# A hybrid decoder layer on one core: two more blocks of the up projection written into the fixed order, and the first down weights loaded into slots

## The chip, the core and the metric

The kernel runs on one core of a Trainium2 chip. The core has five engines that run side by side, each with its own list of instructions: TensorE (PE in the profile: matmuls, with its weight loads in a column PEld), VectorE (DVE), ScalarE (ACT), GpSimd (POOL) and SyncE (SP, here only a queue that issues transfers). Transfers are issued from the queues of SP, ACT and POOL. The metric is the device time of one execution in microseconds (us).

## The reference

One layer: a mixer (mLSTM heads and a causal convolution group, one output projection) and a causal ConvFFN, each between norms, with six modulation rows worked out from a condition vector. Batch 1, 512 positions, width 1024, all float32. The change lies in the ConvFFN:

```
u = rms_norm(x, ffn_pre_g) * (1.0 + sc2) + sh2
up = causal_dwconv(u @ ffn_up, ffn_conv_w, ffn_conv_b)     # 1024 -> 2 x 2816, 3 taps along the positions
a, gt = split(up, 2)
f = (silu(gt) * a) @ ffn_down                              # 2816 -> 1024
x = x + g2 * rms_norm(f, ffn_post_g)
```

## The kernel before, in words

**Numbers in two parts.** TensorE multiplies fp32r operands, so each operand is split into a high part (a copy to fp32r) and a low part (the rest), and each product is three matmuls: high x high, high x low, low x high (`mm3`, L186). A weight tile of 128 x 512 is split in one of two ways: `w_split` (L164) has ACT copy the high part and POOL subtract it for the low part (L170, L171); `added_split` (L1074) has ACT copy the high part, ACT copy it again with scale -1 into the low part (L1077, L1078), and a transfer issued by POOL add the source into the low part (L1079).

**Up projection.** The 2816 columns of each half are 22 units of 128 columns; unit i has a value half (a) and a gate half (g). Units 0 to 7 are plain: 48 matmuls of 512 columns into two PSUM banks (`plain_unit`, L1119). A unit's weights are one raw tile of 128 x 2048, loaded by SP into one of two raw places. From unit 8 on, units go in pairs, one pair a block (m = 4 to 10). The even unit i is computed by a Strassen-Winograd scheme with seven half-size products: sums of weight quarters a11, a12, a21, a22 (p1, p7, p5, p6, then p2, p3, p4) against sums of token quarters (t1 to t4, made once by `token_forms`, L1046, and kept in slots). TensorE's order in a block is written out: the first products p1, p7, p5, p6 into banks X, Z and W (48 matmuls of 256 columns), the value half of the odd unit j (24 of 512), the last products p2, p3, p4 (36 of 256), the gate half of j (24 of 512). Between the first and the last products, `between` (L1099) adds up X, Z and W: two copies on ACT and four operations on VectorE. It needs W, and the last products need it.

**Behind each half** comes a convolution with three taps (`conv3`, L992: one operation on ACT, two on VectorE), which reads the bank and so sets when it is free again; then `unit_out` (L1125: silu on ACT, product on VectorE) writes the half of a tile F. With both units of a pair done, `form_sums` (L1016) and `form_parts` (L1026) make the sums that the down projection multiplies, split them into four slots and spill the rest to memory (L1030, L1031). The first four pairs of sums go out to memory whole (`own_out`, L1138, four transfers from ACT's queue) and come back before the down projection needs them (`reload`, L1254).

**What sets the order.** SP's and TensorE's lists follow the program text. On ACT, VectorE and POOL a list scheduler with a timing model picks the order, except within `in_order()` (L49), where each of these engines keeps the order of the text; instructions from outside may still be put between those of the list. The list with `in_order()` for the up projection begins at L1173 and covers blocks 4 to 10. Before it, the plain units 0 to 7 with their sums (m = 0 to 3, L1150 to L1160) are left to the scheduler; behind it, so is the down projection.

**Places.** `slots` has 44 tiles of 128 x 512 that the scheduler hands out as they come free; `wpool` has 20 for split weights; `raws` two raw places; `mmbank` four PSUM banks, `cvbank` two, `atbank` two. Block 4's X and Z take two of the four mm banks, and unit 9's halves the two cv banks.

**Down projection.** Also Winograd, over 11 groups m of weights (order 4 to 10, then 0 to 3: `ORDER`, L1037). `load1` (L1288) loads three quarters of a group, in one transfer of 768 KB, `forms1` (L1292) makes three sums on VectorE, splits four tiles and writes one sum to memory for later. Groups 0 and 1 go into the raw places, 2 and 3 into the place of the up projection's activations `u2h` (`wd_raw`, L1275; tile `more`). The first phase multiplies p1, p5, p7, p6 of each group (`prod1`, L1331), six matmuls of 512 columns each; p5 and p7 take the mm banks, p6 the cv banks, so p7 wants the banks of unit 20 and p6 those of unit 21.

Of the kernel before, what the change touches and what calls it, by code (L numbers as in the profile page):

```python
# [52 lines left out]
def decoder_layer(ctx, tc, w_glu0, x, xT, c, adaT, vecs, w_glu, w_qko, w_v0, w_v, w_out, w_up, w_down, out):  # L53
# [33 lines left out]
    def mmbank(name):  # L87
        return psum.tile([P, T], F32, tag="mm", bufs=4, name=name)
# [1058 lines left out]
    def open_F(m):  # L1147
        Fs[m] = vpool.tile([P, 2 * T + 8], F32, tag="vh", name=f"F{m}")

    for m in range(MS):  # L1150
# [6 lines left out]
        form_sums(m, Fs[m])  # L1157
        form_parts(m, Fs[m])
        if m < SPILLED:
            own_out(m)  # L1160
    up_load(2 * MS, (0, 2, 3, 1))
    up_load(2 * MS + 1, range(4))
# [7 lines left out]
    def value_part(i, n):  # L1170
        return added_split(places(i)[n], f"wup{i}_{n}")

    with in_order():  # L1173
# [5 lines left out]
        V.tensor_tensor(out=a21, in0=a21, in1=a22, op=ALU.add)  # L1179
        weight_form(i, "p7", a11)  # L1180
        weight_form(i, "p5", a21)
        V.tensor_tensor(out=a11, in0=a22, in1=a11, op=ALU.subtract)
        weight_form(i, "p6", a11)
        value = [value_part(i + 1, n) for n in range(2)]
        before = None
        for m in range(MS, NM):
            i, j = 2 * m, 2 * m + 1
            more_to_come = m + 1 < NM
            open_F(m)
            banks = first_products(i)  # L1190
            pa = plain_half(cvbank(f"up{j}_0"), value, 0)
            s4 = slot(f"s4_{m}")
            V.tensor_tensor(out=s4, in0=a12, in1=a11, op=ALU.subtract)
            weight_form(i, "p2", a12, added_split)
            weight_form(i, "p4", a22)
            if before:
                bj, ba, bg = before
                bg = conv3(bg, NF + bj, f"fg{bj}")
# [4 lines left out]
            if before:  # L1203
                unit_out(bj, ba, bg, Fs[m - 1])
            gate = [value_part(j, 2)]
            if before:
                form_sums(m - 1, Fs[m - 1])
# [4 lines left out]
            if before:  # L1212
                form_parts(m - 1, Fs[m - 1])
# [45 lines left out]

    pairs = pairs[SPILLED:]  # L1260
    g2_d = [g2_d[m] for m in ORDER]
    w_down = [w_down[m] for m in ORDER]


    M1 = NM - 2
    M2 = NM - 3
# [8 lines left out]
    def wd_raw(m, n):  # L1275
        return raws.tile([P, 2048], F32, tag="raw", name=f"wd{n}_{m}") if m % 4 < 2 else more[:, m % 2, :]

    def parts(r, names):
        out = {}
        for name, b in names:  # L1280
            hi, lo = wpool.tile([P, T], F32R, tag="w", name=f"{name}h"), wpool.tile([P, T], F32R, tag="w", name=f"{name}l")
            split(r[:, b * T : (b + 1) * T], hi, lo)
            out[name[:2]] = (hi, lo)
        return out

    loaded = {}

    def load1(m):  # L1288
        loaded[m] = r = wd_raw(m, 1)
        nc.sync.dma_start(r[:, T:], w_down[m][:, T:])  # L1290

    def forms1(m):  # L1292

        r = loaded.pop(m)
        t3, b11, b12, b22 = (quarter(r, b) for b in range(4))
        V.tensor_tensor(out=t3, in0=b22, in1=b12, op=ALU.subtract)
        V.tensor_tensor(out=b12, in0=b12, in1=b11, op=ALU.subtract)
        V.tensor_tensor(out=b22, in0=b22, in1=b12, op=ALU.subtract)
        w = parts(r, [(f"b1_{m}", 1), (f"t1_{m}", 2), (f"t3_{m}", 0), (f"t2_{m}", 3)])
        nc.sync.dma_start(t2_d[m], b22)  # L1300
        return w

    def load2(m):
        loaded[m] = r = wd_raw(m + NM, 2)
        nc.sync.dma_start(r[:, :T], w_down[m][:, :T])
        nc.sync.dma_start(r[:, T : 2 * T], w_down[m][:, 3 * T :])
        nc.sync.dma_start(r[:, 2 * T : 3 * T], t2_d[m])

    def forms2(m):

        r = loaded.pop(m)
        behind_turn(V.tensor_tensor(out=quarter(r, 2), in0=quarter(r, 0), in1=quarter(r, 2), op=ALU.subtract))
        return parts(r, [(f"b2_{m}", 0), (f"b4_{m}", 1), (f"t4_{m}", 2)])

    def load_g2(m):
# [19 lines left out]
            mm3(ps[q], part(form, q), w1[m][w], m == 0, m == NM - 1)  # L1335

    G2A = 3
    w1, w2, g2 = {}, {}, {}
    for m in range(3):
        load1(m)  # L1340
    for m in range(SPILLED):
        reload(m)
    for m in range(NM):
        w1[m] = forms1(m)
        if m + 3 < NM:
            load1(m + 3)
        else:
# [189 lines left out]
```

## Time and profile before

| | |
|---|---|
| median of 3 runs | 795.73 us (791.24 to 796.72) |
| the profiled execution's own time | 790.3 us |
| its span, first to last instruction | 788.6 us |
| mean granted TensorE clock | 0.990 |
| busy: PE, DVE, ACT, POOL | 760.1, 644.0, 443.8, 381.0 us |
| memory read, written | 117.42 MB, 15.61 MB |

A line of the timeline or of a list of waits reads: start in us, duration in us, engine, line of the program, operation, out<-in by the program's names (buffer numbers left out), shapes, count, and in brackets how long the engine stood idle before it and what ended that. A line of a view by stretches reads: the stretch, its length, then busy us and count of PE, PEld, DVE, ACT and POOL, the granted TensorE clock as a share of full speed, the mean busy share of the 16 DMA engines (it can pass 1), and GB/s. A line on transfers reads: out<-in, issuing queue, count, KB each, median us from issue to landing. The up projection's names: `up` a plain bank, `upx`, `upz`, `upw` the banks X, Z, W, `fa6c` and `fg6c` the convolutions of unit 6's value and gate half, `wup_p3l` the low part of form p3, `s` the difference a12 - a11 (s4), `wups` the raw up weights of the blocks; `wd` and `wdmore` raw down weights, `b_0h`, `t_0h` parts of down group 0, `fl_1b` reloaded sums.

### The profile page before, as it was taken

What the parts mean: (1) busy time and instruction counts of PE and PEld (TensorE: products, weight loads), DVE (VectorE), ACT (ScalarE), POOL (GpSimd) and SP (SyncE); (2) the same over time, 40 slices, a digit from 0 to 9 for tenths busy, and PEclk for the clock granted to TensorE, in tenths of its full rate; (3) what the DMA queues carried; (4) which work ended last, traced back from release to release, by engine and by line L of the source; (5) the groups of instructions that cost most, each with busy time, mean ns of one, the idle gap of its engine ahead of it and who ended that gap; (6) DMA issues with size and microseconds to landing.
All of it is one profiled execution on the core that took longest, in us unless ns stands there. A gap on an engine that the chain in (4) does not pass through costs nothing.

```text
span 788.6 us, 11540 instructions
## 1 busy us (share of the span) xinstructions
PE 760.1 (96%) x3961; PEld 649.0 (82%) x3961; DVE 644.0 (82%) x1039; ACT 443.8 (56%) x846; POOL 381.0 (48%) x331
## 2 busy tenths in 40 slices
PE   7999999999999999999999999879999999799996
PEld 5788898778888789888889988769999888588885
DVE  6978999999999857738867598767889866899995
ACT  5447275777675356752435444556667755455762
POOL 2029587796796643553923387344555645100001
PEclk9999999999999999999999999989999999999999
DMA  9983214122031551519754344478998969978872
GB/s 328 366 283 134 82 57 182 56 81 107 28 134 59 186 182 54 209 59 315 273 187 143 138 167 129 151 193 212 240 238 196 207 169 253 384 261 249 291 254 106
DMA packets 52095, 144.80 MB, mean 184 GB/s; under 512 B 6050, under 2 KB 7490, under 8 KB 47940
## 3 DMA queue, kind: packets, MB, share of 16 engines
q1 hardware_dynamic: 30420, 96.18, 35.6%
q10 hardware_dynamic: 14288, 32.68, 11.9%
q0 software_dynamic: 7328, 15.21, 9.4%
q8 instruction: 31, 0.51, 0.3%
q14 instruction: 28, 0.23, 0.1%
HBM read 117.42 MB, written 15.61 MB: 169 GB/s over the span
## 4 chain that ended last, share of the span: by engine, by line
PE 46%; DVE 36%; DMA 6%; ACT 5%; issue 4%; POOL 1%; ACTq 0%; DVEq 0%; POOLq 0%
DVE cv L731 10%; PE p L1384 4%; PE glu L189 3%; PE glu L190 3%; PE glu L188 3%; PE p L188 2%; PE p L189 2%; PE p L190 2%; DMA wup_p3l<-s 2%; PE mixa L188 2%; PE mixa L190 2%; PE mixa L189 2%; PE mixb L189 2%; PE mixb L188 2%; PE mixb L190 2%
## 5 line engine op out<-in xcount | busy, mean ns | idle before, releaser
L731 DVE SCALAR_TENSOR_TENSOR cv<-gt,cvw,cv 128x505 f32<-128x505 f32 (+24 forms) x200 | 137.2, 728 | 2.3 <-ACT cv L719 1.1
L685 POOL TENSOR_TENSOR ro2r<-ro2t,mhalf 128x1 f32<-128x1 f32 x1 | 0.6, 559 | 97.3 <-DVE ro2t L683 97.3
L727 POOL TENSOR_TENSOR cs<-cs,cs 128x510 f32<-128x510 f32 (+3 forms) x32 | 41.8, 1306 | 0.3
L725 ACT ACTIVATE cs<-gt,cvw 128x511 f32<-128x511 f32 (+4 forms) x40 | 27.5, 718 | 6.2 <-POOL cs L727 2.8
L188 PE MATMUL up<-u2h,wup_0h 128*128 128x512 f32 (+1 forms) x72 | 25.7, 357 | 0.4 <-DVE fa5c L997 0.4
L189 PE MATMUL up<-u2l,wup_0h 128*128 128x512 f32 (+1 forms) x72 | 25.7, 357 | 0.2 <-DVE u2l L910 0.2
L171 POOL TENSOR_TENSOR wglu_0l<-wglu,wglu_0h 128x512 fp32r<-128x512 f32 x4 | 5.2, 1308 | 41.9 <-ACT wglu_0h L170 41.9
L190 PE MATMUL up<-u2h,wup_0l 128*128 128x512 f32 (+1 forms) x72 | 25.5, 354 | 0.0
L171 POOL TENSOR_TENSOR wqko_1024l<-wqko,wqko_1024h 128x512 fp32r<-128x512 f32 x12 | 15.5, 1294 | 18.5 <-ACT wqko_1024h L170 13.0
L155 DVE SCALAR_TENSOR_TENSOR junk<-ada,cb 128x1024 bf16<-128x1024 f32 x12 | 18.8, 1567 | 3.8 <-DMA ada<-in_adaT 3.7
L155 DVE SCALAR_TENSOR_TENSOR junk<-spare,cb 128x1024 bf16<-128x1024 f32 x12 | 19.0, 1583 | 3.2 <-DMA spare<-in_adaT 3.0
L188 PE MATMUL qko<-uh,wqko_1024h 128*128 128x512 f32 x48 | 20.6, 430 | 0.0
L188 PE MATMUL qko<-uh,wqko_0h 128*128 128x512 f32 x48 | 20.2, 420 | 0.0
L276 DVE SCALAR_TENSOR_TENSOR junk<-ada,cb 128x1024 bf16<-128x1024 f32 x16 | 19.5, 1218 | 0.1
L171 POOL TENSOR_TENSOR wo_512l<-wo,wo_512h 128x512 fp32r<-128x512 f32 x8 | 12.9, 1617 | 13.2 <-ACT wo_512h L170 13.2
L171 POOL TENSOR_TENSOR wqko_0l<-wqko,wqko_0h 128x512 fp32r<-128x512 f32 x12 | 16.6, 1381 | 5.0 <-ACT wqko_0h L170 5.0
L190 PE MATMUL qko<-uh,wqko_1024l 128*128 128x512 f32 x48 | 18.8, 392 | 0.0
L171 POOL TENSOR_TENSOR wo_1024l<-wo,wo_1024h 128x512 fp32r<-128x512 f32 x8 | 11.6, 1451 | 14.9 <-ACT wo_1024h L170 14.9
L190 PE MATMUL qko<-uh,wqko_0l 128*128 128x512 f32 x48 | 18.8, 391 | 0.0
L189 PE MATMUL qko<-ul,wqko_1024h 128*128 128x512 f32 x48 | 18.7, 390 | 0.0
L189 PE MATMUL qko<-ul,wqko_0h 128*128 128x512 f32 x48 | 18.7, 390 | 0.0
L171 POOL TENSOR_TENSOR wqko_512l<-wqko,wqko_512h 128x512 fp32r<-128x512 f32 x12 | 16.9, 1412 | 3.6 <-ACT wqko_512h L170 3.6
(1216 smaller groups left out, 3151.3 us busy)
## 6 DMA issues: line engine op xcount, KB each, us to landing
wups<-in_w_up SPq DMA_DIRECT2D x56, 256.0 KB, 5.3
wqko<-in_w_qko SPq DMA_DIRECT2D x12, 1024.0 KB, 4.8
ada<-in_adaT ACTq DMA_DIRECT2D x20, 512.0 KB, 5.1
ada<-in_adaT SPq DMA_DIRECT2D x16, 512.0 KB, 7.7
wo<-in_w_out SPq DMA_DIRECT2D x8, 1024.0 KB, 4.9
wup<-in_w_up SPq DMA_DIRECT2D x8, 1024.0 KB, 4.7
spare<-in_adaT ACTq DMA_DIRECT2D x12, 512.0 KB, 7.4
wd<-in_w_down SPq DMA_DIRECT2D x6, 768.0 KB, 4.9
```

The costliest lines, as they stand in the source:

```text
L155: t = V.scalar_tensor_tensor(out=junk, in0=r, scalar=1.0, in1=cb, op0=ALU.mult, op1=ALU.mult, accum_out=mod[:, i : i + 1])
L171: (eng or G).tensor_tensor(out=lo[:, :n], in0=src, in1=hi[:, :n].bitcast(F32), op=ALU.subtract)
L188: PE.matmul(ps, a[0], b[0], start=start, stop=False)
L189: PE.matmul(ps, a[0], b[1], start=False, stop=False)
L190: PE.matmul(ps, a[1], b[0], start=False, stop=stop)
L276: V.scalar_tensor_tensor(out=junk, in0=first[k][:, i * D : (i + 1) * D], scalar=1.0, in1=cb, op0=ALU.mult, op1=ALU.mult, accum_out=part[k] ...
L685: G.tensor_tensor(out=r, in0=t, in1=mhalf[:, :1], op=ALU.pow)
L725: S.activation(t[:, d:], cvx[j][:, : T - d], AF.Copy, scale=w(CK - 1 - d))
L727: G.tensor_tensor(out=side[:, d:], in0=side[:, d:], in1=t[:, d:], op=ALU.add)
L731: last_tap[0] = V.scalar_tensor_tensor(out=cp[:, d:], in0=cvx[j][:, : T - d], scalar=w(CK - 1 - d), in1=cp[:, d:], op0=ALU.mult, op1=ALU.add)
L1384: PE.matmul(ps[q], x, y, start=False, stop=m == NM - 1 and i == 2, skip_group_check=True)
```

## The change

Three things are changed.

1. The pair m = 3 (units 6 and 7) leaves the part given to the scheduler. Its matmuls stay where they were; its convolutions, silu, products, sums and splits are now items of the `in_order()` list, between the weight forms of unit 8 and in block 4, in the places that other blocks have for the pair before. Unit 7 takes the two cv banks in place of mm banks. The spill `own_out(3)` moves behind the weight forms p7 and p5 of the next block.
2. The weights of units 4 to 7 are split by `added_split` in place of `w_split`.
3. The down projection's groups 0, 1 and 2 are loaded within the list: group 0 in block 9, into two slots and the two halves of a tile of the pool `adas`; groups 1 and 2 in block 10 behind the first products, each into four slots, by three transfers of 256 KB (three of the four slots are loaded, the fourth holds a sum). `forms1` is cut in two, the three sums (`forms1`) and the split with the write to memory (`parts1`). The sums of group 0 stand ahead of `between` of block 10, its split behind `form_parts`; the sums of group 1 follow, and its split stands behind unit 20's product. Groups from 2 on are formed in the down projection's loop as before.

```
     def plain_unit(i):
         if i < NE:
             return early[i]
-        pieces = w_load(w_up[i], f"wup{i}")
-        return [plain_half(mmbank(f"up{i}_{half}"), pieces, half * KT) for half in range(2)]
+        if i < 4:
+            pieces = w_load(w_up[i], f"wup{i}")
+        else:
+            r = raws.tile([P, 2048], F32, tag="raw", name=f"wup{i}")
+            nc.sync.dma_start(r, w_up[i])
+            pieces = [added_split(quarter(r, q), f"wup{i}_{q}") for q in range(4)]
+        bank = cvbank if i == SUNITS[0] - 1 else mmbank
+        return [plain_half(bank(f"up{i}_{half}"), pieces, half * KT) for half in range(2)]
...
+    def load1(m, q=None):
+        if q is None:
+            r = wd_raw(m, 1)
+            nc.sync.dma_start(r[:, T:], w_down[m][:, T:])
+            q = [quarter(r, b) for b in range(4)]
+        else:
+            for b in range(1, 4):
+                nc.sync.dma_start(q[b], quarter(w_down[m], b))
+        loaded[m] = q
+
+    def forms1(m):
+        t3, b11, b12, b22 = loaded[m]
+        V.tensor_tensor(out=t3, in0=b22, in1=b12, op=ALU.subtract)
+        V.tensor_tensor(out=b12, in0=b12, in1=b11, op=ALU.subtract)
+        V.tensor_tensor(out=b22, in0=b22, in1=b12, op=ALU.subtract)
+
+    def parts1(m):
+        r = loaded.pop(m)
+        w1[m] = parts(r, [(f"b1_{m}", 1), (f"t1_{m}", 2), (f"t3_{m}", 0), (f"t2_{m}", 3)])
+        nc.sync.dma_start(t2_d[m], r[3])
...
             pa, pg = plain_unit(i)
-            unit_out(i, conv3(pa, i, f"fa{i}"), conv3(pg, NF + i, f"fg{i}"), Fs[m])
+            if m < MS - 1:
+                unit_out(i, conv3(pa, i, f"fa{i}"), conv3(pg, NF + i, f"fg{i}"), Fs[m])
+            elif i % 2 == 0:
+                even = pa, pg
...
         weight_form(i, "p5", a21)
+        ea = conv3(even[0], i - 2, f"fa{i - 2}")
         V.tensor_tensor(out=a11, in0=a22, in1=a11, op=ALU.subtract)
         weight_form(i, "p6", a11)
+        eg = conv3(even[1], NF + i - 2, f"fg{i - 2}")
         value = [value_part(i + 1, n) for n in range(2)]
-        before = None
+        unit_out(i - 2, ea, eg, Fs[MS - 1])
+        before = i - 1, conv3(pa, i - 1, f"fa{i - 1}"), pg
...
             banks = first_products(i)
+            if not more_to_come:
+                for n in (1, 2):
+                    load1(n, [slot(f"wd1_{n}_{b}") for b in range(4)])
...
             form_sums(m - 1, Fs[m - 1])
+            if not more_to_come:
+                forms1(0)
             between(i, *banks)
...
             form_parts(m - 1, Fs[m - 1])
             if m == NM - 2:
                 send_rows(3 * KT, KT)
+                early_raw = adas.tile([P, D], F32, tag="ada", name="wd1_0")
+                load1(0, [slot("wd1_0t"), early_raw[:, :T], early_raw[:, T:], slot("wd1_0b")])
...
+            else:
+                parts1(0)
+                forms1(1)
             va = conv3(pa, j, f"fa{j}")
...
+            if m - 1 < SPILLED:
+                own_out(m - 1)
             X, Z, _ = banks
             last_products_up(X, Z, sforms[i])
...
             unit_out(i, vx, vz, Fs[m])
+            if not more_to_come:
+                parts1(1)
```

In the down projection's loop, the three calls of `load1` ahead of it go, and `forms1(m)` and `parts1(m)` run for m > 1 alone.

More of the change, by code (lines that the diff above doesn't have):

```diff
@@ L1148, in open_F, with wd_raw, parts @@
         Fs[m] = vpool.tile([P, 2 * T + 8], F32, tag="vh", name=f"F{m}")
+    w_down = [w_down[m] for m in ORDER]
+    loaded = {}
+    def wd_raw(m, n):
+        return raws.tile([P, 2048], F32, tag="raw", name=f"wd{n}_{m}") if m % 4 < 2 else more[:, m % 2, :]
+    def parts(r, names):
+        out = {}
+        for name, b in names:
+            hi, lo = wpool.tile([P, T], F32R, tag="w", name=f"{name}h"), wpool.tile([P, T], F32R, tag="w", name=f"{name}l")
+            split(r[b], hi, lo)
+            out[name[:2]] = (hi, lo)
+        return out
+    def load1(m, q=None):
[16 more added lines that the diff above has]
+        nc.sync.dma_start(t2_d[m], r[3])
+    w1 = {}
     for m in range(MS):
@@ L1195, in decoder_layer @@
             weight_form(i, "p4", a22)
-            if before:
-                bj, ba, bg = before
-                bg = conv3(bg, NF + bj, f"fg{bj}")
+            bj, ba, bg = before
+            bg = conv3(bg, NF + bj, f"fg{bj}")
             weight_form(i, "p3", s4, added_split)
@@ L1202, in decoder_layer @@
                     up_load(n + 2, (q,))
-            if before:
-                unit_out(bj, ba, bg, Fs[m - 1])
+            unit_out(bj, ba, bg, Fs[m - 1])
             gate = [value_part(j, 2)]
-            if before:
-                form_sums(m - 1, Fs[m - 1])
+            form_sums(m - 1, Fs[m - 1])
+            if not more_to_come:
+                forms1(0)
             between(i, *banks)
@@ L1273, in decoder_layer @@
     kept = upool.tile([P, 5, 3 * HT], F32, tag="ul", name="g2kept")
[L1275 to L1301, printed above, removed]
     def load2(m):
-        loaded[m] = r = wd_raw(m + NM, 2)
+        r = wd_raw(m + NM, 2)
+        loaded[m] = [quarter(r, b) for b in range(3)]
         nc.sync.dma_start(r[:, :T], w_down[m][:, :T])
@@ L1311, in forms2 @@
         r = loaded.pop(m)
-        behind_turn(V.tensor_tensor(out=quarter(r, 2), in0=quarter(r, 0), in1=quarter(r, 2), op=ALU.subtract))
+        behind_turn(V.tensor_tensor(out=r[2], in0=r[0], in1=r[2], op=ALU.subtract))
         return parts(r, [(f"b2_{m}", 0), (f"b4_{m}", 1), (f"t4_{m}", 2)])
@@ L1337, in decoder_layer @@
     G2A = 3
-    w1, w2, g2 = {}, {}, {}
-    for m in range(3):
-        load1(m)
+    w2, g2 = {}, {}
     for m in range(SPILLED):
@@ L1343, in decoder_layer @@
     for m in range(NM):
-        w1[m] = forms1(m)
+        if m > 1:
+            forms1(m)
+            parts1(m)
         if m + 3 < NM:
```

10 lines of the change are left out of this document (4 added, 6 removed).

## The prediction

> **What bounds the kernel now.** I read the busy shares first, then a table of stretches cut at the starts of the up projection's blocks (TensorE's timeline gives those), with the granted clock in the column PEclk, then TensorE's waits in them.
>
> ```profile
> span 788.6 us, 11540 instructions
> PE 760.1 (96%) x3961; PEld 649.0 (82%) x3961; DVE 644.0 (82%) x1039; ACT 443.8 (56%) x846; POOL 381.0 (48%) x331
> ...
> core 0: us, PE busy (x) PEld busy (x) DVE busy (x) ACT busy (x) POOL busy (x), PEclk, DMA share, GB/s
> ...
> 508.10:542.29 34.19, 26.04 (x133) 23.33 (x133) 21.30 (x33) 18.41 (x33) 13.95 (x13) 0.85 0.76 179
> 542.29:563.29 21.00, 21.00 (x133) 19.09 (x132) 17.68 (x29) 14.91 (x27) 11.73 (x11) 1.00 0.95 240
> ...
> 605.29:627.22 21.93, 21.26 (x133) 19.14 (x132) 20.00 (x32) 16.14 (x30) 11.92 (x12) 1.00 0.88 195
> ...
> 648.33:670.90 22.57, 21.23 (x133) 19.01 (x132) 14.50 (x26) 12.74 (x23) 12.16 (x18) 1.00 0.87 239
> 670.90:682.45 11.55, 7.49 (x25) 5.06 (x24) 9.11 (x15) 4.75 (x8) 2.20 (x4) 0.85 1.02 403
> 682.45:781.70 99.25, 99.25 (x439) 82.05 (x437) 91.05 (x158) 56.05 (x109) 1.66 (x3) 1.00 0.73 249
> ```
>
> TensorE is the bound: 96% busy, and from 682.45 us to the end phase it is never idle. An undisturbed block of the up projection (block 5, the second row of the table) takes 21.00 us. The first block after the plain units, block 4, has the same 133 matmuls and takes 34.19: 13.19 too much. The last, block 10, takes 22.57: 1.57 too much. The first group of the down projection takes 11.55 us; it has 24 matmuls, and 99.25 / 439 is 0.226 us each, so 5.43 would do: 6.12 too much. These are the places that the change touches. TensorE's waits in them:
>
> ```profile
> 497.14 0.47 PE L188 MATMUL up<-u2h,wup_0h 128*128 128x512 f32 x1 [0.38 <-DVE fa5c L997]
> 511.96 0.36 PE L1086 MATMUL upz<-t3h,wup_p7h 128*128 128x256 f32 x1 [2.26 <-DVE fg6c L997]
> 526.44 0.44 PE L1086 MATMUL upx<-u2h,wup_p2h 128*128 128x256 f32 x1 [2.97 <-DVE upx L1106]
> 532.58 0.39 PE L1086 MATMUL upx<-u2h,wup_p3l 128*128 128x256 f32 x1 [2.93 <-DMA wup_p3l<-s]
> 661.04 0.36 PE L1086 MATMUL upx<-u2h,wup_p2h 128*128 128x256 f32 x1 [1.33 <-ACT b_0h L1013]
> 675.44 0.47 PE L188 MATMUL p<-t_0h,fh 128*128 128x512 f32 x1 [1.66 <-DVE fa20c L997]
> 677.36 0.77 PE L188 MATMUL p<-t_0h,fh 128*128 128x512 f32 x1 [0.98 <-ACT t_1h L1013]
> 681.68 0.47 PE L188 MATMUL p<-t_0h,fh 128*128 128x512 f32 x1 [1.42 <-DVE fg21c L997]
> ```
>
> Block 4: 2.26 + 2.97 + 2.93 = 8.16 us idle; the other 5.03 is matmuls at a granted clock of 0.85 (busy 26.04 for work of 21.00). First group: 1.66 + 0.98 + 1.42 = 4.06 idle, 2.06 slow clock. The lost clock comes with the waits and should go with them. [...]
>
> **Why they wait.** For block 4:
>
> ```profile
> 501.41 0.74 DVE L997 SCALAR_TENSOR_TENSOR fg5c<-up,vec,fg5c 128x510 f32<-128x510 f32 x1
> 508.52 0.33 ACTq L1141 DMA_DIRECT2D own<-fl  x1
> 509.49 0.76 ACT L995 ACTIVATE fg6c<-up,vec 128x512 f32<-128x512 f32 x1
> 521.02 0.69 DVE L1193 TENSOR_TENSOR s<-wups 128x512 f32<-128x512 f32 x1
> 522.24 0.63 ACT L1077 ACTIVATE wup_p3h<-s 128x512 fp32r<-128x512 f32 x1 [1.94 <-DMA g2d<-ysq]
> 523.99 0.90 POOL L1079 DMA_DIRECT2D wup_p3l<-s  x1 [9.48 <-ACT wup_2h L1077]
> 524.60 0.37 ACT L1103 ACTIVATE p<-upw 128x256 f32<-128x256 f32 x1
> SPq L1069 <- DVE s L1193: 51.0, 6, 20.4
> ```
>
> The scheduler mixed units 6 and 7 into the written-out order badly. fg6c reads unit 6's bank, which Z of block 4 takes over, and ACT reaches it at 509.49, behind the spill of units 4 and 5's sums. The difference s4 (L1193) runs at 521.02, behind all of units 6 and 7 and their sums; p3's pieces, the copies of X and W (524.60) and `between` follow it, and SP's queue of weight loads stood up to 20.4 us behind it.
>
> ```profile
> 656.17 0.43 DVE L1024 TENSOR_TENSOR ysq<-F,ysum 128x256 f32<-128x256 f32 x1
> 659.53 0.69 DVE L1296 TENSOR_TENSOR wd<-wd 128x512 f32<-128x512 f32 x1 [2.60 <-DMA wd<-in_w_down]
> 660.48 0.42 DVE L1106 TENSOR_TENSOR upx<-upx,u 128x256 f32<-128x256 f32 x1
> 673.34 0.69 DVE L1296 TENSOR_TENSOR wd<-wd 128x512 f32<-128x512 f32 x1 [5.33 <-DMA fl_1b<-own]
> 673.09 0.63 ACT L1013 ACTIVATE b_1h<-wd 128x512 fp32r<-128x512 f32 x1 [6.62 <-DMA wd<-in_w_down]
> 674.55 0.74 DVE L997 SCALAR_TENSOR_TENSOR fa20c<-upx,vec,fa20c 128x510 f32<-128x510 f32 x1
> ```
>
> At the seam to the down projection VectorE stands 2.60 us inside `between`, and 5.33 us inside the convolution of unit 20, each time at a subtraction on down weights that had not landed (the second wait is put down to a reload that came last, but ACT's copy of the same group waited for `wd` itself until 673.09). Banks X, Z and the two of unit 21 come free late, and the group's products p7 and p6 want them.
>
> **The change, part by part.** (1) Unit 7 goes to the cv banks. The wait of 0.38 at 497.14 goes, and block 4's X and Z take unit 5's banks, whose last convolution step ends at 502.15 (first row above). The wait of 2.26 goes. A block's 84 narrow matmuls take 21.00 less 48 x 0.226, so 0.12 us each: 5.8 us for the first products (48), 5.4 for a plain half (24), 4.3 for the last products (36), 5.4. Unit 9's first half now wants unit 7's value bank, 5.8 us into the block; that bank has been full since 497.1 + 5.4 = 502.5.
>
> (2) Units 6 and 7 are written into the order: fa6 after p7 and p5, fg6 after p6, then two value parts, fa7, s4, the pieces p2 and p4, fg7, p3. Unit 7 ends at 508.10 less 0.4, so 507.7; fg7 (0.76 on ACT, 1.5 on VectorE) is then the last thing that s4's successors queue behind, and s4 itself is ahead of it: about 509 where it was 521. p3's two copies follow at 509 to 510.5, its accumulating DMA is issued at about 511 (0.90) and lands 6.5 us later by the first row of the next fence: 518.5. TensorE wants it at 507.7 + 5.8 + 5.4 + 1.4 = 520.3. `between`: silu and product of unit 7 to 512.5, sums to 514, the copies and four operations to 516; wanted at 519. The margins are 2 to 3 us, the loads compete, and I leave 1.0 us of stall in this block. SP's loads for block 5 start about 11 us earlier, as the block does.
>
> (3) The spill of sums 3 (four DMA issues of about 0.33 us on ACT, by the spill row above) moves behind the weight forms of the next block, where ACT has about 6 of 21 us free (14.91 busy in block 5). Nothing of it lies on the path.
>
> (4) Weights of units 4 to 7 get their low part by a second ACT copy and an accumulating DMA:
>
> ```profile
> wup_p3l<-s POOLq DMA_DIRECT2D x7, 256.0 KB, 6.5
> wup_3l<-wups POOLq DMA_DIRECT2D x7, 256.0 KB, 6.9
> L1078 ACT ACTIVATE wup_0l<-wups x7: 613/616/634, 507.6 to 644.1; 128x512 fp32r<-128x512 f32 x7
> L171 POOL TENSOR_TENSOR wup_1024l<-wup,wup_1024h x6: 1287/1304/1742, 393.9 to 488.2; 128x512 fp32r<-128x512 f32 x6
> 484.77 1.74 POOL L171 TENSOR_TENSOR wup_0l<-wup,wup_0h 128x512 fp32r<-128x512 f32 x1
> 440.00:497.00 57.00, 56.76 (x303) 48.92 (x301) 48.74 (x56) 25.25 (x42) 35.69 (x23) 1.00 0.39 134
> wd<-in_w_down SPq DMA_DIRECT2D x6, 768.0 KB, 4.9
> L170 ACT ACTIVATE wup_p1h<-wups x7: 614/623/633, 493.3 to 639.5; 128x512 fp32r<-128x512 f32 x7
> L1069 SPq DMA_DIRECT2D wups<-in_w_up x56: 327/328/652, 478.9 to 642.0; - x56
> ```
>
> Sixteen copies of 0.62 are 9.9 us more for an ACT that is busy 25.25 of 57; sixteen subtractions of 1.3 to 1.74 leave POOL, sixteen issues of about 0.9 come. Each piece is ready some 5 us later than now (6.9 + 0.9 + 0.6 against up to 1.74 and its queue). The tightest, unit 7's first, was ready at 486.5 and is wanted at 497.1: 10.6 us of cover, and if that cover went, each us late would cost TensorE one. I take 0. The raw places, too, come free some 5 us later; unit 8's loads then start at about 484 instead of 478.9 and are read at 493. Zero again; bounds 0 and 2 us.
>
> (5) Down weights early. load1(0) is issued in block 9 behind the last load of the up weights (642.0) and lands 4.9 us after issue, say 648; forms1(0) runs after the sums of block 10, at 656.6. Groups 1 and 2 go into eight slots, which the forms t1, t2, t3 give back as block 10's first products end, 651 to 654; six loads of 256 KB should be in by 660, and forms1(1) comes near 663. So the waits of 2.60 and 5.33 lose their cause. What is added: forms1(0), three subtractions of 0.69 at about 0.6 each, stands ahead of `between`: 656.6 + 1.9 + three of 0.42 = 659.7, and TensorE wants the bank at 661.04 - 1.33 = 659.7. I charge 0.2. parts1(1), four subtractions, stands ahead of fg21: by adding up VectorE's list from 656.6 (forms, `between`, 2 fl, 4 + 3 + 4 for the groups, 6 for convolutions, one product) I come to the end of fg21 about 26 us after the block's start, and p6's second bank is wanted at 21.0 + 4.8: 0.7. The added waits stand on VectorE with the convolutions of units 20 and 21 behind them, and TensorE's p7 behind those.
>
> **The sum.** 0.4 + 13.2 + 1.6 + 6.1 = 21.3 us recoverable; less 1.0 + 0.2 + 0.7 leaves 19.4. Leftover stalls are short and charged without clock: 1.33 us idle in block 10 came with a busy time of only 21.23. The profiled execution, 790.3 us beside its span of 788.6, would become 770.9. It lies 5.4 below the median of the runs shown, 795.73; the same sum from the median gives **776.3**.
>
> **Rivals.** *B, the seam's wait only changes its name.* If groups 1 and 2 get their slots late, or group 3's load, which like now must wait for the activations' place at the end of unit 21, lands among the reloads and the scheduler has put its subtraction first on VectorE, the 7.7 of the seam stays. For it: DMA share 1.02 at 403 GB/s at the seam. Against: three groups of 768 KB, 2.3 MB, have moved ahead of it, into block 10 (share 0.87) and before. Gain 12 to 13: 783.
>
> *C, transfers set block 4.* The stretch of 34.19 us moved 179 GB/s x 34.19 = 6.1 MB; in 21 us that is 291 GB/s, more than the 240 of block 5, though a part (ada rows, the spill) can slide. If only 240 are had, 25.5 us are needed: 4.5 us come back, with clock perhaps 7. Gain 12 to 15: 782.
>
> *D, nothing comes of it*: the order waits elsewhere for as long; 796.
>
> *E, slower.* With its 13 us gap gone the up projection runs just in time, and every block waits for its p3 piece as block 7 does now (21.93). Share 0.95 in 21.00 us is 19.95 us of transfer; it decides once a block's transfers take over 21, 5% more than now, and to eat 19.4 us and end slower, each of the seven blocks must take 24 us, 20% more. Against: the seam reaches 403 GB/s. At 25 us a block: 7 x 4 - 21.3 is 6.7 us slower, 802. [...]
>
> **How the numbers follow.** Forecast 0.62, B 0.17, C 0.13, D 0.04, E 0.04. Faster by over 1% (about what a measurement of this kernel tells from no change): 0.62 + 0.17 + 0.13 = 0.92; within 1%: 0.04; slower: 0.04. Low end: the profiled execution less all 21.3, 769. High end: the median less 11, the lower end of B, 785. D and E, 0.08, are left out, and the rest is for sizes.
>
> **What would show it.** Block 4, from the first p1 matmul of unit 8 to that of unit 10, takes 21 to 23 us, at a clock of 1.00; s4 (the line of L1193) near 509; no SP wait of 20 us on it; no wait on fg6c. The first group of the down projection takes 5.4 to 7 us; no VectorE wait on `wd` within block 10. Blocks 5 to 9 stay at 21.0 to 22. I am wrong if block 4 keeps over 26 us, if a plain unit waits for its low parts, if blocks 5 to 9 grow past 22, or if TensorE waits at groups 1 to 3 of the down projection.

## The result, and where the time went

The changed kernel takes 782.76 us (781.09 to 784.28, 4 runs), the kernel before 793.56 on the same chip (791.24 to 796.72, 4 runs): a ratio of 0.9861, 95% interval 0.9813 to 0.9909. The profiled execution took 782.49 us, with a span of 780.8 where before had 788.6. The forecast was 776.3; the median moved by 10.8 us where it had 19.4, and the span by 7.8.

The same views as in the prediction, for the changed kernel: the page's first lines, then the stretches, cut at the starts of blocks 4 to 10, of the first two down groups and of what follows.

```profile
span 780.8 us, 11567 instructions
PE 757.5 (97%) x3961; PEld 647.1 (83%) x3961; DVE 642.8 (82%) x1039; ACT 451.2 (58%) x862; POOL 367.3 (47%) x331
```

```profile
505.81:526.81 21.00, 21.00 (x133) 19.09 (x132) 17.63 (x29) 14.15 (x26) 11.79 (x11) 1.00 1.01 248
...
590.59:613.78 23.19, 21.25 (x133) 19.14 (x132) 20.74 (x32) 16.93 (x31) 12.52 (x13) 1.00 0.85 196
...
634.89:656.44 21.55, 21.27 (x134) 18.93 (x132) 18.61 (x32) 12.63 (x23) 10.53 (x15) 1.00 0.97 264
656.44:671.11 14.67, 6.34 (x26) 4.93 (x24) 9.45 (x16) 4.53 (x8) 3.30 (x6) 0.80 0.90 326
671.11:678.64 7.53, 7.53 (x25) 6.05 (x24) 4.50 (x10) 1.81 (x4) 0.55 (x1) 0.71 0.25 88
678.64:774.00 95.36, 94.55 (x415) 77.46 (x413) 84.18 (x143) 54.60 (x106) 1.66 (x3) 1.00 0.70 238
```

Block 4 is mended to the last tenth: 21.00 us at clock 1.00 where it was 34.19 at 0.85. The first down group is worse, 14.67 where it was 11.55, and the second takes 7.53 us without one wait, because the clock granted is 0.71. Set against the forecast's steps, with the stretches before quoted in the prediction:

| stretch | forecast, us | measured, us |
|---|---|---|
| up to block 4 | -0.4 | -2.29 (508.10 to 505.81) |
| block 4 | -12.2 | -13.19 |
| blocks 5 to 9 | 0 | +2.04 (106.04 to 108.08) |
| block 10 | -1.4 | -1.02 |
| first down group | -5.4 | +3.12 |
| from the second on | 0 | +3.54 |
| sum | -19.4 | -7.80 |

TensorE's waits in these stretches, by total:

```profile
PE p L188 <- DVE fg21c L997: 8.3, 1, 8.3
...
PE upx L1086 <- DMA wup_p3l<-s: 1.9, 1, 1.9
...
PE p L189 <- DVE t_2l L1014: 0.8, 1, 0.8
...
PE upx L1086 <- DVE upx L1106: 0.3, 1, 0.3
```

One wait of 8.3 us, on the last convolution of unit 21, makes up most of the 9.2 us by which the first group is longer than its 5.44 us of matmuls; the rest is matmuls at the lower clock (6.34 us busy at 0.80). Of the 3.54 us lost from the second group on, 2.06 stand in the second (7.53 where it was 5.47) and 1.32 in the third (6.76 where it was 5.44), which waits 0.8 us for `t_2l`. VectorE's timeline says why fg21 is late, SP's when the load that it waited for went out:

```profile
658.72 0.69 DVE L1014 TENSOR_TENSOR t_1l<-wd,t_1h 128x512 fp32r<-128x512 f32 x1
663.39 0.69 DVE L1183 TENSOR_TENSOR wdmore<-wdmore 128x512 f32<-128x512 f32 x1 [3.98 <-DMA wdmore<-in_w_down]
...
665.81 0.74 DVE L997 SCALAR_TENSOR_TENSOR fg21c<-up,vec,fg21c 128x511 f32<-128x511 f32 x1
...
668.19 0.69 DVE L1183 TENSOR_TENSOR wd<-wd 128x512 f32<-128x512 f32 x1 [0.44 <-DMA wd<-in_w_down]
668.80 0.74 DVE L997 SCALAR_TENSOR_TENSOR fg21c<-up,vec,fg21c 128x510 f32<-128x510 f32 x1
...
674.31 0.69 DVE L1183 TENSOR_TENSOR wd<-wd,wd 128x512 f32<-128x512 f32 x1
```

```profile
629.16 4.73 SPq L1177 DMA_DIRECT2D wd<-in_w_down  x6
...
656.63 0.33 SPq L1173 DMA_DIRECT2D wdmore<-in_w_down  x1
```

`wdmore` is group 3: its load is issued at 656.63, when unit 21 has read the activations whose place it takes. VectorE stands 3.98 us at its first sum, with fg21 behind it, and at 668.19 it forms group 4's before fg21's last step. Group 2, wanted first, is formed last, at 674.31 (the row with two `wd` inputs). Its weights had long been there: groups 1 and 2 were issued from 629.16 on, by 633.9, and no transfer of L1177 took over 9.2 us to land.

### The profile page after: what moved, and what is told of

Same layout as the page of the kernel before. It is cut to its first block, busy times and chain, and to the rows that moved or that the text cites. A ratio compares the mean times of both kernels' runs of the same rounds, so it can differ in the third digit from the quotient of the medians.

```text
span 780.8 us, 11567 instructions
## 1 busy us (share of the span) xinstructions
PE 757.5 (97%) x3961; PEld 647.1 (83%) x3961; DVE 642.8 (82%) x1039; ACT 451.2 (58%) x862; POOL 367.3 (47%) x331
## 3 DMA queue, kind: packets, MB, share of 16 engines
q0 software_dynamic: 9632, 19.40, 12.5%
## 4 chain that ended last, share of the span: by engine, by line
PE 58%; DVE 28%; DMA 5%; ACT 4%; issue 3%; POOL 1%; ACTq 0%; SPq 0%; DVEq 0%; POOLq 0%
DVE cv L731 10%; PE up L189 5%; PE up L190 4%; PE up L188 4%; PE p L1415 4%; PE glu L189 3%; PE glu L188 3%; PE glu L190 3%; PE p L189 2%; PE p L188 2%; PE p L190 2%; PE glu L316 2%; PE mixa L190 2%; PE mixa L188 2%; PE mixa L189 2%
## 5 line engine op out<-in xcount | busy, mean ns | idle before, releaser
L727 POOL TENSOR_TENSOR cs<-cs,cs 128x510 f32<-128x510 f32 (+3 forms) x32 | 41.7, 1304 | 0.3
L171 POOL TENSOR_TENSOR wqko_1024l<-wqko,wqko_1024h 128x512 fp32r<-128x512 f32 x12 | 15.6, 1297 | 18.4 <-ACT wqko_1024h L170 12.9
L171 POOL TENSOR_TENSOR wo_512l<-wo,wo_512h 128x512 fp32r<-128x512 f32 x8 | 12.9, 1615 | 13.6 <-ACT wo_512h L170 13.6
L190 PE MATMUL qko<-uh,wqko_512l 128*128 128x512 f32 x48 | 18.7, 389 | 0.0
```

Source lines behind the costliest of these rows:

```text
L171: (eng or G).tensor_tensor(out=lo[:, :n], in0=src, in1=hi[:, :n].bitcast(F32), op=ALU.subtract)
L190: PE.matmul(ps, a[1], b[0], start=False, stop=stop)
L727: G.tensor_tensor(out=side[:, d:], in0=side[:, d:], in1=t[:, d:], op=ALU.add)
```

## The experiments

**Theory T**: the head's gain (block 4) and the seam's loss (first down groups) are independent; the seam is lost to the order in which the scheduler put the later groups' sums on VectorE, ahead of what TensorE wants next. The rivals: the transfers or the engines' work at the seam are too much whatever the order (S); group 2's place comes free too late (P). A row per run; the stretches are read from TensorE's starts in each profile, "seam on" is from the first matmul of the down projection to the span's end.

| kernel | ratio to before, 95% interval | span | block 4 | blocks 4 to 10 | group 1st, 2nd | seam on |
|---|---|---|---|---|---|---|
| before | 1 | 788.6 | 34.19 | 162.8 | 11.55, 5.5 | 117.7 |
| changed | 0.9861 (0.9813 to 0.9909) | 780.8 | 21.00 | 150.6 | 14.67, 7.53 | 124.4 |
| 1 up part | 0.9831 (0.9791 to 0.9871) | 778.1 | 21.30 | 152.9 | 10.77, 7.06 | 118.5 |
| 2 down part | 1.0022 (0.9997 to 1.0047) | 794.8 | 35.51 | 164.6 | 14.59, 6.14 | 122.9 |
| 3 convolution first | 0.9851 (0.9809 to 0.9893) | 781.6 | 21.00 | 152.2 | 7.01, 5.47 | 122.5 |
| 4 POOL splits | 0.9903 (0.9868 to 0.9938) | 784.5 | 22.51 | 154.7 | 14.42, 6.62 | 123.2 |
| 5 unit 7 on mm banks | 0.9855 (0.9833 to 0.9878) | 779.5 | 21.00 | 150.5 | 13.75, 6.38 | 122.3 |
| 6 place | 0.9913 (0.9881 to 0.9945) | 785.2 | 21.00 | 150.2 | 18.81, 7.41 | 127.0 |
| 7 order | 0.9761 (0.9737 to 0.9785) | 774.5 | 20.99 | 149.5 | 7.00, 5.45 | 117.3 |
| 8 place and order | 0.9783 (0.9756 to 0.9810) | 772.0 | 21.01 | 149.6 | 7.01, 5.45 | 116.3 |
| 9 and group 3 in a raw place | 0.9771 (0.9745 to 0.9796) | 772.7 | 21.00 | 150.8 | 7.02, 5.44 | 115.8 |
| 10 order carried on | 0.9804 (0.9776 to 0.9832) | 777.9 | 21.00 | 150.3 | 7.01, 5.45 | 119.3 |
| 11 late down weights in order | 0.9820 (0.9795 to 0.9844) | 778.9 | 21.00 | 152.4 | 11.37, 7.69 | 119.8 |

### 1 and 2: the two halves of the change

Run 1 is the changed kernel without its third part (no early down weights); run 2 is the kernel before with the third part alone.

```diff
-            if not more_to_come:
-                for n in (1, 2):
-                    load1(n, [slot(f"wd1_{n}_{b}") for b in range(4)])
...
-                load1(0, [slot("wd1_0t"), early_raw[:, :T], early_raw[:, T:], slot("wd1_0b")])
...
+    for m in range(3):
+        load1(m)
```

> The change without its part 3: units 6 and 7 are in the list, units 4 to 7 are split by accumulating transfers, but the down weights are loaded and formed as before. Theory T (the lost time at the seam comes from the early down weights: group 2's sums have no free slot, so groups 3 and 4 come first on VectorE and the last convolution, fg21, waits behind a load): block 4 takes 21.0 us as in the changed kernel, and the seam is that of before (block 10 22.6 us, first group 11.5, second group 5.4), so the span is about 776.6 us, 4 us below the changed kernel, and 14 below before. Rival R (the seam is late because block 4 no longer gives the transfers a pause, so the backlog reaches the seam): first group again 14 us or more, second over 7, span near 781.

> Part 3 of the change alone on the kernel before: down weights early, units 4 to 7 as before. Theory T: block 4 again 34 us, first and second group of the down projection 14 and 7 us with a wait on fg21 near 8 us; span about 792 to 793, 4 us slower than before. Rival R: with the pause of block 4 back the seam is good, first group 6 us, span about 782 (788.6 less some 7).

The up part alone has the head (block 4 at 21.30 us) and a seam on of 118.5 us, the down part alone a block 4 of 35.51 and the same 8.3 us at fg21, so the two are independent: the medians, 12.9 us faster and 2.4 slower than the kernel before, add up to 10.5, where the whole change has 10.8. Theory T missed in sizes: run 1's second group takes 7.06 us where T had 5.4, and the spans, 778.1 and 794.8, lie 1.5 to 2 us past T's. Rival R falls in run 2, and in run 1 by the first group, 10.77 us where R had 14. The third part is worth nothing on its own, and on top of the up part it doesn't pay: it takes 2.2 us out of blocks 4 to 10 and costs 5.9 from the seam on.

### 3: fg21 put ahead of the later groups' sums

```diff
+        if m > 1:
+            tc.add_manual_dep(op.ins, last_step[0].ins.name, ..., reason="order on VectorE")
```

> The changed kernel with one edge of order more: the sums of groups 2 and later may not stand ahead of the last step of fg21 on VectorE. Theory T: the wait on fg21 falls from 8.3 us to under 1, but group 2's sums still stand behind those of groups 3 and 4 and their loads, so TensorE waits some 8 to 10 us at group 2's t parts instead; span within 2 us of the changed kernel's 780.8. Rival S (fg21's place alone costs the time): the wait goes, nothing takes its place, span about 771 to 772.

The first two groups fall to 7.01 and 5.47 us, and the third takes 14.64. TensorE's longest wait and the one left on fg21, the stretches, and a row of VectorE's timeline:

```profile
PE p L188 <- ACT t_2h L1015: 5.5, 1, 5.5
...
PE p L188 <- DVE fg21c L997: 1.3, 1, 1.3
```

```profile
659.11:666.12 7.01, 5.69 (x25) 4.43 (x24) 5.93 (x10) 4.54 (x8) 2.93 (x6) 1.00 1.03 384
666.12:671.59 5.47, 5.47 (x25) 4.50 (x24) 1.89 (x4) 0.00 (x0) 0.92 (x2) 1.00 0.97 344
671.59:686.23 14.64, 8.47 (x26) 6.16 (x25) 14.09 (x27) 9.51 (x19) 0.00 (x0) 0.77 0.57 198
```

```profile
669.70 0.69 DVE L1185 TENSOR_TENSOR wd<-wd 128x512 f32<-128x512 f32 x1 [3.90 <-DMA wd<-in_w_down]
```

fg21 was only the first that queued behind the wrong sums. Group 2's pieces, still formed behind groups 3 and 4, are next, and the gain is handed back one group later. VectorE had 1.89 us of work in the second group, so it isn't short of time there: it stands 3.90 us at the load of group 4, with group 2's sums behind it. Theory T had the place and the span (781.6) right and the sizes not: 1.3 us are left at fg21 where it had under 1, and the wait at group 2 is 5.5 us where it had 8 to 10.

### 6, 7 and 8: place by order

The place: the sums of groups 1 and 2 go to two halves of a tile already there. The order: fg21's last step ahead of group 2's sums, and the sums of groups 3 and later behind group 2's last split. Runs 6, 7 and 8 have the first, the second, and both.

```diff
-                    load1(n, [slot(f"wd1_{n}_{b}") for b in range(4)])
+                    load1(n, [early_raw[:, (n - 1) * T : n * T]] + [slot(f"wd1_{n}_{b}") for b in range(1, 4)])
...
+        for last in [last_step["fg21"] if m == 2 else last_step["group2"]] if m > 1 else []:
+            tc.add_manual_dep(op.ins, last.ins.name, ..., reason="order on VectorE")
```

> The changed kernel with one edit: the sums t3 of down groups 1 and 2 get a fixed place (the two halves of a tile already there) in place of slots; no order is set. Theory T (a wrong order on VectorE costs; the late slot is only what drove group 2's sums to the end): with the place alone VectorE's list still has sums of groups 3 and 4 ahead of fg21, TensorE's wait on fg21 stays at 7 us or more and the span at 778 to 784. Rival P (the late slot is the whole cause): the wait falls below 2 and the span is 770 to 774.

> The changed kernel with the order of the run with place and order, but without its fixed place: fg21's last step ahead of group 2's sums, the sums of groups 3 and later behind group 2's last split, the sums t3 of groups 1 and 2 in slots as in the change. It is the fourth corner of place by order: neither 780.8 us of span, place alone 785.2, both 772.0. Theory T2 (only the order costs; the late slot is what made the scheduler put group 2 last, and costs next to nothing by itself once the order is set): first group 6.5 to 8.5 us, second 5.5 to 8, span 771 to 774. Rival (the slot really comes free late, so that group 2's sums wait for it and the second group's t_2 pieces are late whatever the order): a wait of 3 to 6 us on t_2 in the second or third group, span 776 to 780.

> The changed kernel with three edits at the seam: the sums t3 of down groups 1 and 2 get a fixed place (the two halves of a tile already there) in place of a slot that comes free late; the last step of unit 21's gate convolution stands ahead of group 2's sums on VectorE; and the sums of groups 3 and later stand behind group 2's last split there. Theory T (the seam was lost because sums that wait for group 3's late load stood ahead of fg21 on VectorE, and because group 2's own sums stood last, behind a late slot): the wait of TensorE on fg21 goes from 8.3 to below 1.5 us and no wait over 1.5 takes its place; the first down group takes 5.5 to 7.5 us (14.67 in the changed kernel), the second 5.5 to 7, the blocks before stay as they are; span 770 to 773 where the changed kernel had 780.8, ratio to the kernel before 0.971 to 0.976. Rival S (the transfers of the early weights and the work of the splits are what fills the seam, whatever the order on VectorE): a wait of 4 to 8 us comes up at another name, as it did when only fg21 was put forward; span 778 to 782.

The place alone makes it worse: TensorE waits 12.5 us on fg21, and VectorE has group 3's first sum ahead even of unit 20's product:

```profile
665.62 0.69 DVE L1183 TENSOR_TENSOR wdmore<-wdmore 128x512 f32<-128x512 f32 x1 [5.53 <-DMA wdmore<-in_w_down]
666.23 0.69 DVE L1133 TENSOR_TENSOR F<-fa20c,fg20c 128x512 f32<-128x512 f32 x1
```

So rival P falls; the span of 785.2 is a little past what T had. The order alone gives 774.5, just over its bound, with 1.6 us of wait on t_2h in the third group (9.48 us); both give 772.0. Between these two the medians, 776.04 and 775.65, don't tell. The waits and the stretches of run 8:

```profile
PE p L189 <- DVE t_3l L1016: 2.2, 2, 1.7
...
PE p L188 <- DVE fg21c L997: 1.3, 1, 1.3
```

```profile
655.70:662.71 7.01, 5.69 (x26) 4.43 (x24) 6.22 (x11) 4.53 (x8) 2.74 (x5) 1.00 1.00 369
662.71:668.16 5.45, 5.45 (x26) 4.51 (x24) 5.45 (x11) 3.47 (x6) 0.55 (x1) 1.00 1.02 403
668.16:673.60 5.44, 5.44 (x26) 4.50 (x24) 3.52 (x7) 2.92 (x6) 0.00 (x0) 1.00 0.91 364
673.60:682.02 8.42, 6.21 (x25) 4.27 (x24) 8.10 (x15) 5.10 (x10) 0.00 (x0) 1.00 0.67 215
```

The transfers run at 364 to 403 GB/s in the first three groups, and TensorE waits there for nothing but fg21, so rival S falls too. Two waits of 2.2 us in all, the longest 1.7, were left in the fourth group, against T's word.

### 9 and 10: the fourth group

Run 9 loads group 3 earlier, into a raw weight place, in the list behind group 1's split. Run 10 carries the order on instead: every group's sums behind the last split of the group before.

```diff
-        for last in [last_step["fg21"] if m == 2 else last_step["group2"]] if m > 1 else []:
+        for last in [last_step["fg21" if m == 2 else f"group{m - 1}"]] if m > 1 else []:
```

> The changed kernel with place and order, and with group 3 loaded into a raw weight place, issued within the list behind group 1's split, in place of the activations' place behind unit 21 (group 4 takes the other raw place, and the activations' place serves groups 5 and 6). Theory T (what is left of the seam with place and order is group 3's load, which still waits for the end of unit 21: TensorE's 2.2 us on t_3l and its lost clock): that wait goes, the fourth group takes 5.5 to 6.5 us in place of 8.42, span 769 to 771. Rival (the transfers of the seam are full, so the wait moves to group 4's or the reloads' pieces): span 771.5 to 774.

> The changed kernel with place and order, and with the order carried on: the sums of every down group m from 3 on stand on VectorE behind the last split of group m - 1 (before: behind group 2's last split for all of them). In the run with place and order VectorE waited 2.24 us on group 5's load with a subtraction that stood ahead of group 3's splits, and TensorE waited 2.2 us on t_3l; moving group 3's load only moved this wait (1.73 us on group 5's load, TensorE 1.7). Theory T (a subtraction of a later group, put ahead of a split that is wanted sooner, is what holds TensorE at each group): TensorE's wait on t_3l falls to 0.5 us or less, the fourth group takes 5.4 to 6.5 us in place of 8.42, span 769 to 770.5. Rival (with every sum behind the split of the group before, the sums come too late and the wait moves to a t or b piece of group 4, 5 or 6): waits of 1.5 us or more there, span 771.5 to 775.

In run 9 the wait kept its name (t_3l, 1.7 us in two waits, the group 7.92 us) though group 3 came early, against T, and the span is the rival's: VectorE stood 1.73 us at group 5's first sum, which was placed ahead of group 3's splits. The medians, 776.87 and run 8's 775.65, don't tell the two apart. VectorE in run 9, then in run 8, which has the same picture:

```profile
674.63 0.69 DVE L1186 TENSOR_TENSOR wdmore<-wdmore 128x512 f32<-128x512 f32 x1 [1.73 <-DMA wdmore<-in_w_down]
```

```profile
673.92 0.69 DVE L1186 TENSOR_TENSOR wd<-wd 128x512 f32<-128x512 f32 x1 [2.24 <-DMA wd<-in_w_down]
...
676.34 0.68 DVE L1016 TENSOR_TENSOR t_3l<-wdmore,t_3h 128x512 fp32r<-128x512 f32 x1
```

Run 10 takes that wait away, and the fourth group takes 5.44 us, as T had it:

```profile
676.48:681.92 5.44, 5.44 (x26) 4.50 (x24) 5.31 (x10) 2.83 (x7) 0.00 (x0) 1.00 0.61 228
718.00:734.22 16.22, 12.67 (x46) 9.30 (x45) 14.54 (x26) 9.45 (x22) 0.00 (x0) 0.89 0.71 238
```

```profile
719.68 0.69 DVE L1350 TENSOR_TENSOR wd<-wd 128x512 f32<-128x512 f32 x1 [3.76 <-DMA wd<-t2d]
```

Yet the span is 777.9, where T had 769 to 770.5 and the rival named groups 4 to 6. Neither was right. The 3.0 us came back at the start of the second phase (the second row), where VectorE stands 3.76 us at a reload (`wd<-t2d`, its timeline's row) and TensorE waits 1.8, 1.1 and 0.6 us: from the sixth group to the end run 10 takes 6 us more than run 8. It also reached the down projection 2.9 us later, 2.2 of them already at block 4, up to where each engine has the same instructions in the same order in both.

The traces say where the reload's delay began. The sixth group starts at 687.4 us in both runs. From there, VectorE at the first sum of the last group and SP behind it, in run 8:

```profile
701.70 0.68 DVE L1186 TENSOR_TENSOR wdmore<-wdmore 128x512 f32<-128x512 f32 x1
```

```profile
706.62 0.33 SPq L1197 DMA_DIRECT2D t2d<-wdmore  x1
707.06 0.37 SPq L1343 DMA_DIRECT2D wd<-in_w_down  x1
```

And in run 10:

```profile
707.15 0.68 DVE L1186 TENSOR_TENSOR wdmore<-wdmore 128x512 f32<-128x512 f32 x1
```

```profile
711.50 0.33 SPq L1197 DMA_DIRECT2D t2d<-wdmore  x1
711.93 0.37 SPq L1343 DMA_DIRECT2D wd<-in_w_down  x1
```

In run 10 the last group's sums may start only behind the last split of the group before, and they do so 5.45 us later than in run 8. SP's queue writes one of them to memory and issues the next loads of the second phase behind that write, 4.9 us later. So the order carried on stands at the head of this chain; no run undid it to prove that nothing else adds to it. The intervals of runs 8 and 10 overlap, so the medians, 775.65 and 777.96, leave it open which is faster.

### 11: the early loads, once the order is right

Run 1 with an order: group 1's sums behind fg20, those of later groups behind fg21.

> The changed kernel without its third part (down groups 0 to 2 are loaded and formed behind the list, as before), and with an order on VectorE there: the sums of group 1 behind the last step of unit 20's gate convolution, those of groups 2 and later behind the last step of unit 21's. This asks what the early loads are worth once the order is right. Theory T (order is what cost most, but VectorE's and ACT's work on two whole groups at the seam has to stand somewhere): the waits on fg20 and fg21, 1.0 and 2.9 us without the order, go below 1, the first group takes 8 to 11 us and the second 6 to 8, span 775 to 778 where it was 778.1 without the order. Rival O (order alone, the early loads are worth nothing): first group 5.5 to 7.5, span 770 to 773, as with the early loads in order.

Rival O falls: with the weights late the order brings nothing that the runs tell (ratio 0.9820 beside run 1's 0.9831, span 778.9 beside 778.1). The first group, 11.37 us, fg21's wait, 1.8, and the span lie a little past T's bounds. So the early weights seem to be worth something, but only with the order: beside run 8, 2.7 us in blocks 4 to 10, 3.5 from the seam on, and 3.2 of the median. The two intervals still overlap by a little, and run 8 has the place as well.

### 4 and 5: the two edits that the forecast priced near nothing

Run 4 gives units 4 to 7 their POOL subtraction back, run 5 puts unit 7 back on mm banks (the edit shown).

```diff
-        bank = cvbank if i == SUNITS[0] - 1 else mmbank
+        bank = mmbank
```

> The changed kernel with the weights of units 4 to 7 split by POOL's subtraction as before. If part 2 matters little (the prediction charged it 0): plain units at 10.9 us each, block 4 at 21.0 to 22, span within 2 us of the changed kernel. Rival (POOL's subtractions slow VectorE beside them and keep the list late): a wait of over 1 us returns in block 4 or at unit 7, span 2 to 5 us longer.

> The changed kernel with one edit undone: unit 7 takes two of the four mm banks, as before, in place of the two cv banks. Theory of the prediction (the banks are a small term: block 4's X and Z then want the banks of unit 6 and 7's halves, which are free only behind their convolutions): a wait of TensorE for a convolution comes back in block 4, 2 to 5 us in all, block 4 takes 23 to 26 us in place of 21.00, span 783 to 786. Rival (the banks are worth nothing, the written order alone mended block 4): block 4 within 0.5 of 21.0 and the span within 1 us of 780.8.

The banks are worth nothing: block 4 takes 21.00 us and nothing waits for a bank, so the rival was right. The split by transfer is worth something, on the side that the forecast's bounds left out: blocks 4 to 10 take 154.7 us in run 4, in place of 150.6, and s4 comes at 511.91 where the changed kernel has 506.56. Run 4's rival had the cause and the span (784.5) right; the wait of over 1 us came in block 8 (1.8 us for a p3 piece), not in block 4, whose longest is 0.8. VectorE in run 4, and POOL beside it:

```profile
484.41 0.74 DVE L997 SCALAR_TENSOR_TENSOR fg4c<-up,vec,fg4c 128x510 f32<-128x510 f32 x1
...
486.22 1.67 DVE L1056 TENSOR_TENSOR b<-b,b 128x512 f32<-128x512 f32 x1
487.82 1.78 DVE L1128 TENSOR_TENSOR F<-fa4c,fg4c 128x512 f32<-128x512 f32 x1
489.52 1.77 DVE L1014 TENSOR_TENSOR t1l<-b,t1h 128x512 fp32r<-128x512 f32 x1
```

```profile
483.90 1.74 POOL L171 TENSOR_TENSOR wup_0l<-wup,wup_0h 128x512 fp32r<-128x512 f32 x1
485.60 1.75 POOL L171 TENSOR_TENSOR wup_512l<-wup,wup_512h 128x512 fp32r<-128x512 f32 x1
487.30 1.75 POOL L171 TENSOR_TENSOR wup_1024l<-wup,wup_1024h 128x512 fp32r<-128x512 f32 x1
489.02 1.73 POOL L171 TENSOR_TENSOR wup_1536l<-wup,wup_1536h 128x512 fp32r<-128x512 f32 x1
```

Each of the last three VectorE operations ends 0.5 us after a subtraction on POOL has ended; the same t1l takes 0.68 in the changed kernel. Six such operations there (1.12 to 1.78 us each) cost 5.8 us over 0.68 each, about s4's delay of 5.35. The convolution fg4c, which reads the bank `up`, stays at 0.74 beside a subtraction that runs from 483.90 to 485.64. Why some operations are stretched and this one isn't, the rows don't show.

## Why the prediction was right, and where it was wrong

The median, 782.76, lies inside the forecast's range of 769 to 785, but the mechanism held for one half only. Block 4 came as forecast; the first down group, forecast to gain 5.4 us, lost 3.1, and 3.5 more went behind it. In the profile 2.29 us of the gain stand ahead of block 4, where single executions scatter by as much (below): that part is luck. Two of the prediction's own signs of being wrong came up, a block of 5 to 9 past 22 us (block 8) and TensorE's waits at the first down groups.

**Block 4, right.** The order is the cause by what is left over: with the banks undone block 4 takes 21.00 us (run 5), with the splits undone 22.51 (run 4), with the whole up part undone 35.51 (run 2). No run undid the order alone. s4 ran at 506.56, forecast 509:

```profile
506.56 0.68 DVE L1246 TENSOR_TENSOR s<-wups 128x512 f32<-128x512 f32 x1
...
508.83 0.90 POOL L1079 DMA_DIRECT2D wup_p3l<-s  x1
```

The 1.0 us of stall left for this block didn't come, and the clock came back as the waits went (1.00 where it was 0.85).

**(1) The banks, wrong in cause.** "The wait of 2.26 goes" because X and Z take other banks: it goes with the old banks too. In run 5 fg6's last step ends by 504.2 us, and Z's first matmul follows at 508.17 without a wait, so what frees Z's bank in time is fg6's place in the order, part of step (2).

**(4) The splits, mis-sized.** "I take 0", bounds 0 and 2 of loss. It was a gain: without it blocks 4 to 10 take 154.7 us (run 4), where the ten kernels with the split by transfer take 149.5 to 152.9, so 2 to 5 us. The step counted POOL's subtractions as work on POOL alone; the row quoted for it, 1.74 us beside a median of 1304 ns, already showed that something stretched some of them.

**(5) The seam, where it failed.** The sums of group 0 ahead of `between` cost 0.3 us, forecast 0.2. What failed is "I come to the end of fg21 about 26 us after the block's start ... 0.7": it was 669.54 (668.80 + 0.74), 34.7 us after 634.89, and TensorE waited 8.3 us. (The two figures of that sentence, 26 and 21.0 + 4.8, differ by 0.2 and not by 0.7; the slip is small beside this.) The adding up took VectorE's list to be the text's, groups 0 and 1 with fg21 behind them. But the text orders only what stands in the list; group 3's and 4's sums came from outside it and were put in between. Runs 3, 7 and 8 confirm it: with fg21 ahead of those sums the wait is 1.3 us and the first group 7.0. That is rival B by its own condition. Its time, 783, fits partly by chance: B's gain was 12 to 13 us and the measured one is 10.8, but B started from 795.73, where the kernel before had 793.56 beside the change. (The range's high end takes 11 us as B's lower end, where B itself has 12.) What spoke against B, that 2.3 MB had moved ahead of the load, was beside the point: in the changed kernel the load was issued as early as unit 21's end allows and landed within 6.8 us (656.63 to 663.39); what cost was which sum stood first. The slots were wrong as well: the loads of groups 1 and 2 went out 1 to 6 us ahead of block 10's start, not 3 to 6 us behind it, which didn't prevent the wait.

**Blocks 5 to 9** lost 2.04 us, most of it in block 8 (23.19 where it was 21.93; the prediction calls it block 7), where TensorE waits 1.9 us for the p3 piece: a small share of rival E's mechanism. No run tried it, and runs 3 and 6 to 10, with the same order up to there, have 22.0 to 22.9. **Rivals C, D and E** fell: block 4 moves 248 GB/s, not the 291 that C asked for, at 21.00 us.

**Up to block 4** the 2.29 us can't be put down to an edit: block 4 starts between 505.81 and 508.25 in the changed kernel and in runs 3 and 6 to 10, in which every engine has the same instructions in the same order up to there. Spans of single executions that differ by 2 us thus tell little; the stretches tell more.

## What to carry to other kernels

Where an order written by hand ends, the scheduler's begins, and it may put work of the part behind into the part ahead: a list of what an engine will do counts only when the first operations from outside it are placed too, above all those that wait for a late load. Early weights and their order are one edit; here the loads without the order gained nothing that the runs tell (ratio 0.9861 beside run 1's 0.9831, with intervals that overlap), nor did the order without the loads, and both together gave 0.978 of the time before. A wait that is taken away at one group tends to come up at the next, so read the third and the fourth group before calling the first one mended.

## What the runs showed of the hardware

In run 1 the lower clock shows behind the waits and not beside them, and none of TensorE's waits there from 500 us on reaches 3 us. The first down group has 4.57 us of waits, the longest 2.9, and a clock of 1.00; the second has no wait and 0.76:

```profile
659.63:670.40 10.77, 6.20 (x26) 4.27 (x25) 9.21 (x15) 4.86 (x8) 2.20 (x4) 1.00 1.02 402
670.40:677.46 7.06, 7.06 (x26) 5.66 (x25) 6.46 (x12) 3.46 (x6) 0.00 (x0) 0.76 0.99 364
```

In run 8 the fourth group's 2.2 us in two waits left the clock at 1.00 there, and the next group takes 5.45 us, also at 1.00. Beside the 5.44 us of an undisturbed group, the second group takes 1.62 us more in run 1 (7.06) and 2.09 more in the changed kernel (7.53, at 0.71), where nothing waits. So in these two cases a reader finds part of the loss a group later than the waits. What lowers the clock isn't shown.
